# Attention scores by query-tile pairs: two packed 128-row products and four 32-row ones in row groups, reciprocals taken on columns

## The chip, the cores and the metric

The kernel runs on one core of a Trainium2 chip. The metric is the device time of one execution in microseconds (us), lower is better. Before the change it is 2180.84 us, the median of 3 runs (2180.51 to 2181.43).

The core's engines work side by side and meet at semaphores: PE (TensorE) multiplies matrices into PSUM, DVE (VectorE) and ACT (ScalarE) work element by element, POOL (GpSimd) does side work, and SP (SyncE) issues DMAs. Each engine takes its instructions in the order in which they are written.

## The reference

Two layers; each mixes tokens by attention and a convolution and then runs a gated FFN. Sequence 1024, model width 1024, 8 heads. The change is in the attention, whose score of a query and a key has a part of 64 dimensions of its own for each head and a rotary part of 32 dimensions whose key is shared by all heads.

```python
        q = (c_q @ w_uq[l].astype(h.dtype)).reshape(b, s, MLA_HEADS, MLA_NOPE_DIM + MLA_ROPE_DIM)
        q_nope = q[..., :MLA_NOPE_DIM]
        q_rope = _apply_rope(q[..., MLA_NOPE_DIM:], cos_h, sin_h)
        ...
        k_nope = kv[..., :MLA_NOPE_DIM]
        v = kv[..., MLA_NOPE_DIM:]
        k_rope = _apply_rope(p[..., o2:o3], cos, sin)
        y_attn = _mla_attention(q_nope, q_rope, k_nope, k_rope, v)
...
        sc = (jnp.einsum("bqhd,bkhd->bhqk", qn, k_nope)
              + jnp.einsum("bqhr,bkr->bhqk", qr, k_rope))
        p = jax.nn.softmax(sc.astype(jnp.float32) * scale, axis=-1).astype(v.dtype)
        return jnp.einsum("bhqk,bkhd->bqhd", p, v)
```

## The kernel before

Each layer has three stages: `project` (all input projections, rotary embedding, a part of the convolution), `attention`, and `feed` (output projection and FFN). Both layers run the same code, so every place below occurs twice in the program.

**Number format.** To come near float32, a float32 operand is split into an upper and a lower float16 half, and a product is made of three: upper by upper, upper by lower, lower by upper. In the tiles of a head, `q` and `k`, of shape (128, 2, 1024), index 0 and 1 of the middle dimension are the two halves; partitions 0 to 63 hold the head's own part, 64 to 95 the rotary part.

**Tiling of the attention.** A head has 8 query tiles of 128 rows, numbered n = 0 to 63 over the 8 heads. For a tile, `scores` (L1810 on) writes a PSUM tile `s` of 128x1024 (two banks; there are two such tiles) with 6 products of 96 rows by 512 columns (L1818); DVE takes the negated row maximum `mx` (L1820); `expo` lets ACT write the exponentials `p` with the row sums into `sums` (L1828). For every pair of tiles `turn` transposes `p` on PE in blocks of 128x128 into four PSUM tiles `t`, c = 0 to 3, of two blocks for each query tile (L1858); ACT writes the upper half `pt` of each (L1860), DVE the lower half (L1861). A group is two pairs; `values` multiplies its `pt` by the values into a PSUM tile `o`: in steps c = 0 to 3 two full products each (L1880), and with the last step 8 products of 64 columns (L1885) for the lower halves, which go into two column halves of PE. ACT and DVE then write `o` out as `yt` (L1891, L1892).

`sums` (L1901 on) handles the row sums when a head is done: PE transposes them into a PSUM tile `sr` of 8x128 (L1903), DVE takes the reciprocals (L1905), and SP writes them to DRAM and reads them back, spread over 64 partitions (L1906, L1907), for a later multiplication on POOL.

`o`, `t`, `sr` and the value projection's `pv` all come from a ring of four PSUM banks. A new tile in a bank waits until the tile before it in that bank has been read.

**Order.** The program is written out by hand in the order of each engine's queue: the loop over n emits the value products that are due at n, `turn(n)`, `scores(n + 2)`, `expo(n + 1)`, and then what `agenda[n]` holds (side work: late convolution taps, `sums`, casts). So PE works two tiles ahead of the exponentials and one pair ahead of the transposes. The eight value projections (`rows`, L1794, 6 products each) stand among the first tiles, as `ROWS`, `ROW_AT` and `ROW_LATE` say, each followed by two ACT and two DVE writes (L1804, L1807).

**How the operands reach the tiles.** `project` writes the split queries and keys to DRAM (`qd`, `qrd`, `kd`, `krd`) and `load_head` reads a head's tiles back, all on SP's queue (line L153, `move`). Head 0 (`DIRECT = 1`) is copied straight from the SBUF tiles, the rotary query parts `qr` (two tiles, one for each half of the 32 dimensions, heads on partitions) among them. `spills` holds the DRAM writes back until the second query projection; then they are issued one after another, and the loads of head 1 and head 2 stand behind them in SP's queue.

## Time and profile before

| what | value |
|---|---|
| median of 3 runs | 2180.84 us |
| span of the profiled execution, first to last instruction | 2179.0 us |
| busy PE / DVE / ACT / POOL | 2169.7 / 1844.7 / 1456.6 / 537.2 us |
| attention of layer 0, first `s` product to last | 200.07 to about 386.7 us |
| attention of layer 1, first `s` product to last | 1280.91 to 1467.2 us (start of the last) |
| DVE `mx` (L1820) | 128 times, mean 1211 ns |
| ACT `p` (L1828) | 128 times, mean 1120 ns, and 210 ns to read the sums |
| PE `s` (L1818), `t` (L1858) | 768 and 1024 products |

A matmul's duration in the trace is from its start to its modelled end; matmuls that follow each other overlap, so what one costs PE is read from the distance of the starts, or from the chain of work that ended last, which counts overlapping work once. Times are us from the start of the span.

### The profile page before, as it was taken

The page shows a single profiled execution, that of the slowest core. Times are in us where ns is not written, and L with a number is a line of the kernel's source. Part 1 is how long each engine was busy: PE and PEld are TensorE (multiplying, and loading weights), DVE is VectorE, ACT ScalarE, POOL GpSimd, SP SyncE. Part 2 cuts the span into 40 slices and gives each one's busy share as a digit, 9 for nine tenths or more (in the row PEclk, how much of TensorE's full clock was granted, in tenths as well). Part 3 has the DMA queues.
Part 4 walks back from the last instruction along what each step waited for, and adds up shares of the span by engine and source line. Part 5 has one row for each costly group of instructions (what it writes and reads, how often), then busy time and mean ns, then how long its engine had stood idle before and what let it go on. Part 6 is the DMA issues. An engine that isn't in the chain of part 4 may idle for free.

```text
span 2179.0 us, 29766 instructions
## 1 busy us (share of the span) xinstructions
PE 2169.7 (100%) x10722; PEld 1260.7 (58%) x10722; DVE 1844.7 (85%) x2531; ACT 1456.6 (67%) x2183; POOL 537.2 (25%) x534
## 2 busy tenths in 40 slices
PE   9999999999999999999999999999999999999998
PEld 8887665754444444644488876667544444446445
DVE  6989999879998887887859789998898888878877
ACT  6455888746898886554623668886478888865544
POOL 1223777211111111000012355771112111110000
PEclk9999999999999999999999999999999999999999
DMA  6898878754688885554578986886646888856533
GB/s 195 184 187 212 164 152 171 245 163 104 149 244 259 222 261 145 193 178 151 166 177 164 188 207 134 159 186 200 175 100 164 261 241 242 241 141 218 182 111 122
DMA packets 163013, 400.96 MB, mean 184 GB/s; under 512 B 21888, under 2 KB 29936, under 8 KB 162864
## 3 DMA queue, kind: packets, MB, share of 16 engines
q0 software_dynamic: 62528, 145.89, 36.4%
q1 hardware_dynamic: 100048, 252.63, 33.8%
q8 instruction: 84, 1.38, 0.3%
q10 hardware_dynamic: 288, 0.53, 0.1%
q14 instruction: 65, 0.53, 0.1%
HBM read 270.75 MB, written 69.66 MB: 156 GB/s over the span
## 4 chain that ended last, share of the span: by engine, by line
PE 98%; ACT 1%; DVE 1%; issue 0%; DMA 0%; DVEq 0%; ACTq 0%
PE p L1306 36%; PE pd L1551 18%; PE po L1026 7%; PE s L1818 7%; PE t L1858 5%; PE pq L245 3%; PE pa L245 3%; PE o L1880 2%; PE pkv L245 2%; PE pg L245 2%; PE pg L564 2%; PE pn L245 2%; PE o L1885 1%; PE pv L1794 1%; PE pk L245 1%; PE pa L564 1%
## 5 line engine op out<-in xcount | busy, mean ns | idle before, releaser
L1306 PE MATMUL p<-b,w 128*128 128x512 f16 x3696 | 800.0, 379 | 0.2
L1306 PEld LDWEIGHTS <-w 128*128 128x128 f16 x3696 | 358.7, 98 | 431.9 <-issue 0.8
L1551 PE MATMUL pd<-ab,wd 128*128 128x512 f16 (+2 forms) x1920 | 404.2, 373 | 0.0
L1196 POOL DMA_DIRECT2D wu<-in_w_up x176 | 152.2, 879 | 770.2 <-DVE w L1270 581.5
L1551 PEld LDWEIGHTS <-wd 128*128 128x128 f16 x1656 | 161.9, 98 | 179.4 <-issue 0.5
L1818 PE MATMUL s<-k,q 96*128 96x512 f16 x768 | 186.9, 379 | 0.0
L1270 DVE SCALAR_TENSOR_TENSOR w<-wu,wf,w 128x512 f16<-128x512 f32 (+1 forms) x216 | 177.2, 834 | 3.6 <-ACT w L1267 3.6
L1861 DVE SCALAR_TENSOR_TENSOR pt<-t,pt 128x512 f16<-128x512 f32 x256 | 163.0, 676 | 10.0 <-ACT pt L1860 9.0
L1267 ACT ACTIVATE w<-wu,wf 128x512 f16<-128x512 f32 (+1 forms) x216 | 164.8, 781 | 0.1
L1860 ACT ACTIVATE pt<-t 128x512 f16<-128x512 f32 x256 | 139.1, 596 | 32.0 <-PE t L1858 30.0
L1820 DVE TENSOR_REDUCE mx<-s 128x1 f32<-128x1024 f32 x128 | 155.0, 1211 | 1.0 <-PE s L1818 1.0
L1540 ACT ACTIVATE ab<-ac,ds 128x512 f16<-128x512 f32 x108 | 75.5, 717 | 108.7 <-DVE ac L1455 73.0
L1828 ACT ACTIVATE p<-s,mx 128x1024 f32<-128x1024 f32 x128 | 143.3, 1120 | 2.2 <-DVE mx L1820 1.8
L2039 DVE SCALAR_TENSOR_TENSOR conv<-gate,par,conv 128x1009 f32<-128x1009 f32 (+14 forms) x110 | 139.9, 1274 | 3.1 <-ACT conv L659 0.4
L2056 POOL TENSOR_SCALAR late<-gate,par 128x1019 f32<-128x1019 f32 (+13 forms) x99 | 135.5, 1368 | 27.2 <-PE pn L245 13.9
L1858 PE MATMUL t<-ident,p 128*128 128x128 f32 x1024 | 136.6, 275 | 0.9 <-ACT p L1828 0.6
L1858 PEld LDWEIGHTS t<-ident,p 128*128 128x128 f32 x1024 | 116.8, 141 | 34.8 <-issue 7.4
L1766 DVE SCALAR_TENSOR_TENSOR o<-zg,par,o 128x1023 f32<-128x1023 f32 x88 | 112.7, 1281 | 8.9 <-ACT o L1760 7.4
L1314 DVE SCALAR_TENSOR_TENSOR zg<-p,wf,zg 128x512 f32<-128x512 f32 x72 | 54.0, 750 | 71.2 <-PE p L1306 61.6
L1766 DVE SCALAR_TENSOR_TENSOR v<-zv,par,v 128x1023 f32<-128x1023 f32 x88 | 112.1, 1276 | 0.0
L1818 PEld LDWEIGHTS <-q 96*128 96x128 f16 x768 | 74.0, 97 | 64.6 <-issue 2.1
L1541 DVE SCALAR_TENSOR_TENSOR ab<-ac,ds,ab 128x512 f16<-128x512 f32 x108 | 79.9, 748 | 19.2 <-ACT ab L1540 19.2
(2179 smaller groups left out, 3814.1 us busy)
## 6 DMA issues: line engine op xcount, KB each, us to landing
wu<-in_w_up SPq DMA_DIRECT2D x98, 512.0 KB
wu<-in_w_up POOLq DMA_DIRECT2D x176, 256.0 KB, 4.8
sd<-in_w_down SPq DMA_DIRECT2D x44, 512.0 KB
ws<-sd SPq DMA_DIRECT2D x44, 512.0 KB
act<-v SPq DMA_DIRECT2D x36, 512.0 KB
ac<-act SPq DMA_DIRECT2D x72, 256.0 KB
wo<-in_w_o POOLq DMA_DIRECT2D x32, 256.0 KB, 7.7
x_mix<-y SPq DMA_DIRECT2D x32, 256.0 KB
```

Of the source, the lines that this page charges most:

```text
L245: nc.tensor.matmul(ps[:, HALVES[c]], w, x[:, HALVES[c]], start=(k == 0 and s == 0), stop=(k == n - 1 and s == 2))
L1026: self.nc.tensor.matmul(ps, p[:, sl], q[:, cs], start=(k == 0 and t == 0), stop=(k == 3 and t == 2))
L1196: nc.gpsimd.dma_start(out=dst, in_=src, accum_op=ALU.add)
L1267: nc.scalar.activation(out=t, in_=src, func=AF.Copy, scale=scale[f])
L1270: nc.vector.scalar_tensor_tensor(out=t, in0=src, scalar=scale[f], in1=hi, op0=ALU.mult, op1=ALU.subtract)
L1306: nc.tensor.matmul(ps, w[p][:, k * 128:(k + 1) * 128], b[:, q], start=(i in (1, 5, 2) and k == 0 and t == 0), stop=(k == 3 and t == 2), sk ...
L1551: nc.tensor.matmul(ps[t, m][:, cs], w[i, j][p][:, m * 128:(m + 1) * 128], b[:, q, cs], start=(i in (1, 5, 2) and j == 0 and s == 0), stop= ...
L1766: self.nc.vector.scalar_tensor_tensor(out=o[:, a:b], in0=z[:, at + a:at + b], scalar=self.par[l][:, tap:tap + 1], in1=o[:, a:b], op0=ALU.m ...
L1818: nc.tensor.matmul(ps[:, cs], q[0:96, i, qs], k[0:96, j, cs], start=(s == 0), stop=(s == 2))
L1820: nc.vector.tensor_reduce(out=mx, in_=ps, op=ALU.max, axis=AX.X, negate=True)
L1858: nc.tensor.transpose(tp[:, i, qi * 128:(qi + 1) * 128], st["p"][2 * qp + qi][:, kt * 128:(kt + 1) * 128], self.ident)
L1861: nc.vector.scalar_tensor_tensor(out=lo, in0=tp, scalar=P_SCALE, in1=hi, op0=ALU.mult, op1=ALU.subtract)
```

## The change

**The scores.** With three products of 96 rows, a score needs 288 rows. The change lays the same 288 rows out as 128 + 128 + 32. In `q[:, 0]` and `k[:, 0]` stand the upper half of the query's own part twice, against the upper and the lower half of the key; in `q[:, 1]` and `k[:, 1]` the lower half of the own part against the key's upper half (64 rows), and the upper half of the rotary part twice, against the two halves of the rotary key (64 rows). The rest is the lower half of the rotary query against the upper half of the rotary key: 32 rows. Its operands are put on four groups of 32 partitions: `qc` (shared by two heads) holds the query's part four times, `kc` the key's columns 0 to 511 in groups 0 and 2 and 512 to 1023 in groups 1 and 3. The new `scores` handles a pair of tiles: 4 products for the first tile, four 32-row products (two tiles by two column halves, each in its own row group and its own PSUM bank), and, later, 4 products for the second tile. A pair thus has 8 products of 128 rows and 4 of 32 rows where it had 12 of 96 rows.

**The order.** The loop runs over pairs. In an iteration PE gets: value products, first part of the next pair's scores with the four 32-row products, the transposes c = 0, 1, 3, the second tile's scores, value products, the transposes c = 2. The DVE and ACT halves of `turn` (`lower`, `upper`), the maximum (`largest`) and `expo` are placed between them one by one. At the start the value projections stand in three groups around the first pair.

**The reciprocals.** `inverses` takes them on the 128x8 tile of sums before the transposition; ACT copies the transposed tile out of PSUM.

**The operands.** Head 0 takes 12 small copies of rotary parts instead of 2, and one more of its own part; the rotary queries are written to DRAM by head and half in 32 pieces instead of 2; `load_head` issues 12 DMAs instead of 5.

```diff
-        qrd = self.dp.tile([2, HEADS, HALF, 2, T], F16, name=f"qrd{l}")
+        qrd = self.dp.tile([2, HEADS, ROPE, T], F16, name=f"qrd{l}")
...
+            st["kc"] = self.blk(f"kc{l}", F16, (128, 512))
+            for r in range(4):
+                self.move(st["kc"][r * ROPE:(r + 1) * ROPE], krd[0][:, HALVES[r % 2]])
...
                 for h in range(DIRECT):
-                    self.move(heads[h][0][NOPE + i * HALF:NOPE + (i + 1) * HALF], hl[h * HALF:(h + 1) * HALF])
-                spills.append((qrd[i].rearrange("h d p t -> (h d) p t"), hl))
+                    for r, (t, p) in enumerate([(heads[h][0][:, 1], 0)] * 2 + [(heads[h][2][:, h % 2], 1)] * 4):
+                        at = i * HALF + (NOPE + r * ROPE if p == 0 else (r - 2) * ROPE)
+                        self.move(t[at:at + HALF], hl[h * HALF:(h + 1) * HALF, p])
+                for p in range(2):
+                    for h in range(HEADS):
+                        spills.append((qrd[p, h, i * HALF:(i + 1) * HALF], hl[h * HALF:(h + 1) * HALF, p]))
...
+        self.move(q[NOPE:128, 0], qd[h][:, 0])
+        for p in range(2):
+            self.move(k[p * NOPE:(p + 1) * NOPE, 0], kd[h][:, p])
+            self.move(q[NOPE + p * ROPE:NOPE + (p + 1) * ROPE, 1], qrd[0, h])
+        self.move(k[0:NOPE, 1], kd[h][:, 0])
+        self.move(k[NOPE:128, 1], krd.rearrange("p d t -> (p d) t"))
+        for r in range(4):
+            self.move(qc[r * ROPE:(r + 1) * ROPE, h % 2], qrd[1, h])
...
-            for s, (i, j) in enumerate(((0, 0), (0, 1), (1, 0))):
-                for cs in HALVES:
-                    nc.tensor.matmul(ps[:, cs], q[0:96, i, qs], k[0:96, j, cs], start=(s == 0), stop=(s == 2))
+            def whole(e):
+                for i in range(2):
+                    for cs in HALVES:
+                        nc.tensor.matmul(two[e][:, cs], q[:, i, at[e]], k[:, i, cs], start=(i == 0 and e == 0),
+                                         stop=(i == 1 and e == 1), skip_group_check=True)
+
+            def rest():
+                for e in range(2):
+                    for c in range(2):
+                        r = slice((2 * e + c) * ROPE, (2 * e + c + 1) * ROPE)
+                        nc.tensor.matmul(two[e][:, HALVES[c]], qc[r, h % 2, at[e]], kc[r], start=(e == 1),
+                                         stop=(e == 0), skip_group_check=True)
...
+        def inverses(h):
+            nc.vector.reciprocal(out=state[h]["sums"], in_=state[h]["sums"])
...
-            nc.vector.reciprocal(out=rs, in_=pr)
+            nc.scalar.copy(out=rs, in_=pr)
...
+        for pair in range(total // 2 - 1):
+            n, nxt = 2 * pair + 1, pair + 1
+            products(n)
+            begin(nxt)
+            turn(pair, 0)
+            upper(pair, 0)
+            turn(pair, 1)
+            upper(pair, 1)
+            largest(2 * nxt)
+            ends = [rows(tt) for tt in ROWS_LATE.get(n, ())]
+            turn(pair, 3)
+            upper(pair, 3)
+            second.pop(nxt)()
+            lower(pair, 0)
+            largest(2 * nxt + 1)
+            expo(2 * nxt)
+            lower(pair, 1)
...
+            others(n)
+            products(n + 1)
...
+            turn(pair, 2)
+            upper(pair, 2)
+            expo(2 * nxt + 1)
+            lower(pair, 2)
+            lower(pair, 3)
...
+            others(n + 1)
```

Three places show how the queues move. First DVE, head 2 of layer 0, from the maximum of tile 2 to that of tile 4. `mx_2_2` is the maximum of head 2, tile 2; `t_2_03` is pair 0's transposed block c = 3; `pt_10` and `pt_11` are lower halves. Before:

```order
L1820 TENSOR_REDUCE mx_2_2_2260<-s_2_2_2253 128x1
L1861 SCALAR_TENSOR_TENSOR pt_10_2282<-t_2_00_2276,pt_00_2281 128x2x256
L1861 SCALAR_TENSOR_TENSOR pt_10_2282<-t_2_01_2287,pt_00_2281 128x2x256
L1820 TENSOR_REDUCE mx_2_3_2301<-s_2_3_2294 128x1
L1861 SCALAR_TENSOR_TENSOR pt_11_2284<-t_2_02_2310,pt_01_2283 128x2x256
L1861 SCALAR_TENSOR_TENSOR pt_11_2284<-t_2_03_2317,pt_01_2283 128x2x256
L1820 TENSOR_REDUCE mx_2_4_2331<-s_2_4_2324 128x1
```

The same place on DVE after the change (L1854 is the maximum, L1892 the lower half, L1920 `yt`, L1931 the reciprocals):

```order
L1854 TENSOR_REDUCE mx_2_2_2366<-s_2_2_2326 128x1
L1892 SCALAR_TENSOR_TENSOR pt_10_2356<-t_2_00_2350,pt_00_2355 128x2x256
L1854 TENSOR_REDUCE mx_2_3_2379<-s_2_3_2327 128x1
L1892 SCALAR_TENSOR_TENSOR pt_10_2356<-t_2_01_2360,pt_00_2355 128x2x256
L1892 SCALAR_TENSOR_TENSOR pt_11_2358<-t_2_02_2389,pt_01_2357 128x2x256
L1892 SCALAR_TENSOR_TENSOR pt_11_2358<-t_2_03_2368,pt_01_2357 128x2x256
L1920 SCALAR_TENSOR_TENSOR yt_0_1880<-o_1_1_2308,sc_85,yt_0_1880 64x512
L1931 RECIPROCAL sums_1_1974<-sums_1_1974 128x8
L1854 TENSOR_REDUCE mx_2_4_2434<-s_2_4_2412 128x1
```

The second maximum of a pair now stands between the lower halves of c = 0 and c = 1, and the lower half of c = 1 behind it. Second, PE at the transposition of the sums `sr_1`, also in head 2. Before, with the last score product of tile 6 ahead of it:

```order
L1858 MATMUL t_2_12_2380<-ident,p_2_3_2333 128x128 x2
L1858 MATMUL t_2_13_2387<-ident,p_2_2_2303 128x128 x2
L1858 MATMUL t_2_13_2387<-ident,p_2_3_2333 128x128 x2
L1818 LDWEIGHTS q_2_1978
L1818 MATMUL s_2_6_2394<-k_2_1979,q_2_1978 128x512
...
L1903 MATMUL sr_1_2408<-ident,sums_1_1900 8x128
```

After (L1836 are 128-row score products, L1908 value products, L1880 transposes):

```order
L1836 MATMUL s_2_5_2413<-k_2_2045,q_2_2044 128x512
L1908 LDWEIGHTS v_0_1652
L1908 MATMUL o_2_0_2457<-pt_00_2355,v_0_1652 128x512
...
L1880 MATMUL t_2_12_2460<-ident,p_2_2_2381 128x128 x2
L1880 MATMUL t_2_12_2460<-ident,p_2_3_2395 128x128 x2
L1935 MATMUL sr_1_2473<-ident,sums_1_1974 8x128
```

Before, six score products stood between the pair's last transposes and `sr`; now `sr` follows the transposes at once, three steps behind the second tile's scores. In both, `sr_1` takes the bank of `t_2_11`, so it waits for DVE's lower half of c = 1. Third, SP's queue from head 0's rotary copies to head 1's loads. Before:

```order
L153 DMA q_0_1324<-qr_0_1486 16x2048
L153 DMA q_0_1324<-qr_1_1487 16x2048
L153 DMA q_0_1324<-qns_0_1511 64x2048
L153 DMA qrd_81<-qr_0_1486 128x2048
L153 DMA qrd_81<-qr_1_1487 128x2048
L153 DMA qd_80<-qns_0_1511 128x2048
...
L153 DMA qd_80<-qns_3_1585 128x2048
L153 DMA q_1_1694<-qd_80 64x2048
L153 DMA q_1_1694<-qrd_81 16x2048 x2
L153 DMA k_1_1695<-kd_82 64x2048
L153 DMA k_1_1695<-krd_83 32x2048
```

After (`qr` is the rotary query in SBUF, `qns` the head's own part, `qrd` and `qd` their places in DRAM):

```order
L150 DMA q_0_1330<-qr_0_1495 16x1024 x2
L150 DMA qc_0_1329<-qr_0_1495 16x1024 x4
L150 DMA q_0_1330<-qr_1_1496 16x1024 x2
L150 DMA qc_0_1329<-qr_1_1496 16x1024 x4
L150 DMA q_0_1330<-qns_0_1520 64x2048
L150 DMA q_0_1330<-qns_0_1520 64x1024
L150 DMA qrd_81<-qr_0_1495 16x1024 x16
L150 DMA qrd_81<-qr_1_1496 16x1024 x16
L150 DMA qd_80<-qns_0_1520 128x2048
...
L150 DMA q_1_1759<-qd_80 64x2048
L150 DMA qc_0_1329<-qrd_81 32x1024 x4
```

Between the first copy for head 0 and the last load for head 1 there were 14 DMAs; there are now 62.

More of the change, by code (lines that the diff above doesn't have):

```diff
@@ L2012, in attention, with others, begin @@
+        def others(n):
             for f in agenda.pop(n, ()):
                 f()
-            if n == total - 1:
-                early(1, range(2))
-            if n == total:
-                values(2 * HEADS - 1, 0, n)
-                values(2 * HEADS - 1, 1, n)
-                early(1, range(2, 3))
-                values(2 * HEADS - 1, 2, n)
-                values(2 * HEADS - 1, 3, n)
+        def begin(pair):
+            h, p = divmod(pair, 4)
+            if h >= HEADS:
+                return
+            if p == 0:
+                state[h] = {"sums": self.cp.tile([128, 8], F32, name=f"sums{l}_{h}", tag="sums", bufs=3),
+                            "s": {}, "p": {}, "pt": {}, "qk": loaded.pop(h)}
+            second[pair] = scores(pair)
+            if p == 1 and h + 1 < HEADS and h + 1 not in loaded:
+                loaded[h + 1] = load(h + 1)
@@ new lines, in each @@
+        def each(pair, f, *e):
+            if pair < total // 2:
+                f(*e)
+        for tt in ROWS_FIRST:
+            rows(tt)()
+        begin(0)
+        ends = [rows(tt) for tt in ROWS_SECOND]
+        largest(0)
+        second.pop(0)()
+        expo(0)
+        for f in ends:
+            f()
+        largest(1)
+        ends = [rows(tt) for tt in ROWS_THIRD]
+        expo(1)
+        for f in ends:
+            f()
+        others(-1)
+        others(0)
+        for pair in range(total // 2 - 1):
[15 more added lines that the diff above has]
+            lower(pair, 1)
+            for f in ends:
+                f()
+            others(n)
+            products(n + 1)
+            ends = [rows(tt) for tt in ROWS_LATE.get(n + 1, ())]
+            turn(pair, 2)
[3 more added lines that the diff above has]
+            lower(pair, 3)
+            for f in ends:
+                f()
+            others(n + 1)
+            for qi in range(2):
+                state[pair // 4]["p"].pop(2 * (pair % 4) + qi)
@@ L2022, in attention @@
+        pair = total // 2 - 1
+        early(0, range(3))
+        for c in range(4):
+            turn(pair, c)
+            upper(pair, c)
+            lower(pair, c)
+            if c % 2:
+                others(total - 1 + c // 2)
+            if c == 1:
+                early(1, range(2))
+        g = 2 * HEADS - 1
+        values(g, 0, total)
+        values(g, 1, total)
+        early(1, range(2, 3))
+        values(g, 2, total)
+        values(g, 3, total)
         for m in range(2):
```

123 lines of the change are left out of this document (50 added, 73 removed).

## The prediction

> **What bounds the kernel now.** I read the page first, for the engine that ends the work, then the two attention stages by windows, then the chain of waits inside one of them.
>
> ```profile
> PE 2169.7 (100%) x10722; PEld 1260.7 (58%) x10722; DVE 1844.7 (85%) x2531; ACT 1456.6 (67%) x2183; POOL 537.2 (25%) x534
> PE 98%; ACT 1%; DVE 1%; issue 0%; DMA 0%; DVEq 0%; ACTq 0%
> ```
>
> The second line is the chain that ended last: 98% of the span is PE's own work. The windows (us of the stretch, then busy time of PE, PEld, DVE, ACT, POOL, granted clock, DMA share, GB/s) are the start and the middle of layer 0's attention:
>
> ```profile
> 216.00:237.00 21.00, 20.71 (x128) 12.57 (x127) 19.36 (x26) 17.19 (x32) 18.06 (x16) 1.00 0.87 167
> 237.00:370.00 133.00, 133.00 (x829) 80.14 (x828) 121.00 (x156) 109.39 (x195) 96.89 (x82) 1.00 0.80 160
> ```
>
> PE has no gap in 133 us, at the full clock; DVE is busy 121.0 of them (91%). So time leaves this stage only by less work on PE, and only until DVE, or the order in which the engines hand work to each other, becomes the limit. The chain of waits (start, us, what) shows the price of each step on PE, overlaps counted once:
>
> ```profile
> 300.89 1.30 PE s L1818 x6
> ...
> 304.90 0.43 PE o L1880 x2
> 305.33 0.87 PE t L1858 x8
> 306.20 1.30 PE s L1818 x6
> 307.50 0.43 PE o L1880 x2
> 307.93 0.98 PE o L1885 x8
> 308.92 1.02 PE t L1858 x8
> 309.94 1.30 PE s L1818 x6
> ...
> 312.54 1.30 PE s L1818 x6
> ```
>
> One group (two pairs of tiles) takes 312.54 - 300.89 = 11.65 us. A score product of 96 rows costs 1.30/6 = 0.217 us, a value product of 128 rows 0.43/2 = 0.217: the number of rows makes no difference. A transpose costs 0.87/8 = 0.109.
>
> **What the packing saves.** Per pair 12 products of 0.217 become 8 of 0.217 and a group of four with 32 rows. The trace has no 32-row product. The nearest row is L1885: eight products that each use half of PE's columns, in 0.98 us, where eight in sequence would take 1.74. So two halves ran together (4 x 0.217 = 0.87), with 0.11 us lost beside them, and the transposes right behind took 1.02 instead of 0.87: 0.15 more. Changing the division of PE costs 0.26 us a visit here. With the four 32-row products side by side the group costs 0.217 + 0.26 = 0.48 instead of 0.87: 0.39 saved, over 64 pairs **-25.0 us**. Below, a free change of division would save 0.65 a pair, 41.6 in all. Above, four products in sequence and the same change cost 1.13, 0.26 more than now, +16.6 in all. I take 0.39, since the row shows both the overlap and the loss.
>
> The Trainium skill, "TensorEngine Tiling (Array Packing)", Key Properties, says that a change of tiling mode drains TensorE; that speaks against visits as short as these, and the trace agrees, with 0.11 and 0.15 us around L1885. By the skill's "TensorE: Matmul & The Clock Gate", Part 3, four row tiles of 32 rows were measured 3.07 times as fast as in sequence; by that figure the group would be an estimated 4 x 0.217 / 3.07 = 0.28 instead of 0.217, and the sum 4 us higher. No run here shows it yet.
>
> **What the new order adds: two waits on PE.** There are still only two score tiles in PSUM, and now a pair fills both. Counted from E, the end of the second tile's four products:
>
> ```profile
> 306.04 1.46 PE L1818 MATMUL s<-k,q 96*128 96x512 f16 x6
> ...
> 307.67 1.21 DVE L1820 TENSOR_REDUCE mx<-s 128x1 f32<-128x1024 f32 x1
> ```
>
> E of the products in the chain above is 307.50; the maximum starts at 307.67, 0.17 later, and takes 1.21. From a maximum to PE the way leads over the exponential; it lay on the critical chain once, at the start:
>
> ```profile
> 217.37 1.28 DVE pt L1861 x2
> 218.65 1.14 DVE mx L1820
> ...
> 221.13 0.87 PE t L1858 x6
> ...
> 224.61 1.30 PE s L1818 x6
> ```
>
> The maximum has ended at 219.79, PE goes on at 221.13: 1.34 us. So the second tile is free for new scores at E + 0.17 + 1.21 + 1.34 = E + 2.72. That is what two of the next 32-row products wait for (the ones that write the second tile). PE's work before them is two value products (0.43), four transposes (0.44), two value products (0.43), four scores (0.87), the change of division (0.11): 2.28. PE stalls 0.44 us, and everything behind waits with it, since the queue is in order. In every other pair the 8 half products (0.98) stand there too and hide it. So it counts in 16 of a layer's 32 pairs, less 2 at the start and 7 in which the next wait has already taken the time: 7 x 0.44 x 2 layers = **+6.2 us**.
>
> The second wait is that of `sr` for its bank. The tile ahead of it is freed by the lower half of c = 1, which now stands behind the second maximum on DVE: 0.17 + 1.14 (maximum to the next instruction, row 218.65) + 0.68 (L1861 below) + 0.16 (the chain counts a product from the end of the one before; the scores that it has at 306.20 start at 306.04) = E + 2.15. PE has only 0.43 + 0.44 = 0.87 to do before it. It stalls 1.28 us; before, six score products (1.30) stood in between and hid this.
>
> ```profile
> L1861 DVE SCALAR_TENSOR_TENSOR pt<-t,pt 128x512 f16<-128x512 f32 x256 | 163.0, 676 | 10.0 <-ACT pt L1860 9.0
> L1905 DVE RECIPROCAL rs<-sr 8x128 f32<-8x128 f32 x14 | 13.1, 934 | 0.0
> ```
>
> L1905 gives the number of times, 14: 14 x 1.28 = **+17.9 us**. Queued behind `sr` are value products and the next pair's scores, so nothing makes it up. The bounds of both waits are zero, if DVE or ACT come earlier than in my sum, and twice these values. Together they take back nearly all of the 25.0.
>
> The reciprocals themselves leave DVE: 14 x 0.93 = 13.0 us less work there, for 14 that are short, 8 values in a row instead of 128. While PE or the handover limits, DVE's 9% of slack covers them, so I count nothing; were DVE the limit, it would be -13. ACT's 14 new copies of an 8x128 tile are smaller than any L1860 (0.6 us) and have ACT's slack for cover (109.4 of 133 busy); without it they cost up to 8 us.
>
> **The start.** Before, PE ran through it with tiles staggered one by one:
>
> ```profile
> 196.15 4.08 PE pv L1794 x18
> ...
> 204.22 2.74 PE pv L1794 x12
> ```
>
> ```profile
> 200.63 2.44 DVE L1807 SCALAR_TENSOR_TENSOR v<-pv,sc,v 128x256 f16<-128x256 f32 x6
> 206.21 1.63 ACT L1804 ACTIVATE v<-pv,sc 128x256 f16<-128x256 f32 x4
> 207.07 1.67 DVE L1807 SCALAR_TENSOR_TENSOR v<-pv,sc,v 128x256 f16<-128x256 f32 x4 [0.96 <-ACT v L1804]
> ```
>
> Now DVE has, behind tile 0's maximum (203.07 to 204.28, after the x6 row), the lower halves of two value projections, which wait for ACT's upper halves, which stand behind tile 0's exponential (to about 205.4). As in the last two rows that is 0.86 and 1.67 us more: tile 1's maximum starts at about 208.0 and frees PE at 208.0 + 1.21 + 1.34 = 210.55. PE, from 200.23: scores and group 0.87 + 0.48, 12 projections 2.74, scores 0.87, 12 projections 2.74, scores 0.87 = 208.8. It stalls 1.7. The next pair goes the same way with two more projections (maxima at about 212.9 and 214.7, PE free at 217.3 against 216.0): 0.5 and 0.8. About 3.0 us a layer: **+6.0**. Below zero is excluded, as PE had no more than 0.29 us of gaps here to win; above, 5 a layer.
>
> **SP's queue.** PE's timeline has the first scores of each layer, SP's (start, us, what it issues) the DMAs around them, and the list of what SP waits for (us in total, times, longest us) in a window of head 1, one landing:
>
> ```profile
> 200.07 1.25 PE L1818 MATMUL s<-k,q 96*128 96x512 f16 x5
> 1280.91 1.25 PE L1818 MATMUL s<-k,q 96*128 96x512 f16 x5
> ```
>
> ```profile
> 189.66 1.62 SPq L153 DMA_DIRECT2D q<-qr  x2
> 192.45 1.27 SPq L153 DMA_DIRECT2D qrd<-qr  x2
> 201.17 0.49 SPq L153 DMA_DIRECT2D q<-qd  x1
> 208.98 0.76 SPq L153 DMA_DIRECT2D k<-krd  x1
> 1268.84 1.64 SPq L153 DMA_DIRECT2D q<-qr  x2
> ```
>
> ```profile
> SPq L1907 <- DMA sd<-rs: 2.9, 1, 2.9
> ```
>
> The writes to `qrd` take 1.27/2 = 0.63 us per issue. From `q<-qd` to `k<-krd` there are ten loads in 201.17 to 209.74, 0.86 each, with DMA busy (share 0.87). A transfer lands 2.9 us after SP is ready again, some 3.3 after it started. From 189.66 there are now 12 copies (7.6), 2 (1.3), 32 writes (20.2), 4 (2.5) and 12 loads (7.6): the last load is issued at 228.2 and lands near 231.4. Head 1's first scores were at 224.61 with 8 score tiles before them; in the new order value products and half products (1.41) come first, three groups have saved 1.2 and the start has cost 3.0: 227.8, and the 32-row operands, loaded last, are wanted 0.9 later. PE stalls 2.7 us. In layer 1, SP starts 1.66 us earlier relative to the first score (1280.91 - 1268.84 = 12.07 ahead, instead of 200.07 - 189.66 = 10.41): 1.1. Loads of 0.86 would add 12 x 0.23 = 2.8 to both. I take between 3.8 and 9.4: **+5**, and from zero (issues of 0.55 or less) to +32 (all 62 issues of 0.86, 14 more in each layer). Later heads have 20 us of lead for 12 issues, and DMA's share of 0.80 in the middle leaves room; the cost is nothing there.
>
> **The sum**: -25.0 + 6.2 + 17.9 + 6.0 + 5 = +10.1 us on the span of 2179.0: 2189.1. The median is 1.84 above the span, so **2190.9, say 2191 us**.
>
> **Rivals.** (1) *Shorter waits*: the handovers above come from rows in which other work lay between, and half of the two waits would be -12.0: 2179; with none and loads in time 2162. For it: DVE gets 0.93 back at each head. Against it: the chain of a maximum, an exponential and PE is made of durations alone. (2) *Operands late*: all issues at 0.86, +32 instead of +5: 2218. For it: layer 1's loads of before. Against it: the 32 writes are small. It decides once an issue takes over 0.55 us; below that the loads are in time. (3) *No overlap of the 32-row products*: 41.6 more, of which the 6.2 of the first wait is absorbed: 2226. Then the change does not do what it says. For it: no row with row groups. Against it: L1885. (4) *The waits are right and the loads in time*: 2186.
>
> **How the numbers follow.** Around 2191, with (4): 0.44. Shorter waits: 0.17 under 2176.5, and 0.23 between that and 2185.2, where the waits are a little shorter and the loads in time. Late operands 0.10, no overlap 0.06. Within 0.2% (4.4 us, about what a measurement tells from no change) is 2176.5 to 2185.2. Faster 0.17, same 0.23, slower 0.60. The range reaches from 2172 (most of the shorter waits) to 2218 (late operands); the likeliest case alone holds 2185 to 2202.
>
> **What would show it.** Right: in the middle of the attention a group takes 11.6 to 11.8 us as before, PE has gaps ended by DVE's lower half ahead of `sr` and by ACT's `p` ahead of the 32-row products, and the first scores of head 1 end a gap that a DMA ended. The four 32-row products start within some ns of each other. Wrong: no gap on PE and a group of about 10.9 (rival 1); the four 0.2 us apart (rival 3); gaps that a maximum ends where PE had enough to do.

## The result and the profile after

The changed kernel takes 2234.18 us (median of 4 runs, 2232.64 to 2236.86), the kernel before 2181.14 us in the same comparison: 1.0244 times as long, 95% interval 1.0229 to 1.0258. That is 53 us more, where 10 were forecast; the direction was right, the size lies outside the range. The profiled execution's span is 2232.5 us.

The page's line of busy times, the chain that ended last, and the group of the 128-row score products (busy us, mean ns of one, idle us just before them and what ended most of that):

```profile
PE 2164.8 (97%) x10722; PEld 1243.0 (56%) x10722; DVE 1842.1 (83%) x2531; ACT 1454.5 (65%) x2197; POOL 536.4 (24%) x534
PE 86%; ACT 5%; DVE 4%; DMA 3%; issue 2%; SPq 1%; DVEq 0%; ACTq 0%
L1836 PE MATMUL s<-k,q 128*128 128x512 f16 x512 | 134.3, 384 | 31.8 <-DMA k<-kd 26.6
```

PE has hardly less to do than before (2169.7 us), and the chain is no longer PE's alone. One releaser stands out: DMA, 26.6 us, ahead of score products. The same two windows as before (us of the stretch, then busy time of PE, PEld, DVE, ACT, POOL, granted clock, DMA share, GB/s):

```profile
216.00:237.00 21.00, 12.03 (x76) 6.62 (x74) 13.52 (x19) 12.00 (x24) 16.64 (x15) 0.88 1.02 241
237.00:370.00 133.00, 117.72 (x746) 66.60 (x747) 105.49 (x136) 95.80 (x178) 79.19 (x66) 0.94 0.79 168
```

In the first, PE works 12.03 of 21 us, its clock is no longer full, and DMA is fully busy. The list of what PE waited for in layer 0 from the start of the attention on (us in total, times, longest us) names the places:

```profile
PE s L1836 <- DMA k<-kd: 13.7, 1, 13.7
PE sr L1935 <- DVE pt L1892: 6.9, 6, 1.2
PE s L1843 <- ACT p L1862: 3.6, 10, 1.2
PE s L1836 <- DMA k<-krd: 1.8, 1, 1.8
PE sr L1935 <- DVE sums L1931: 1.2, 1, 1.2
PE s L1843 <- DMA qc<-qrd: 1.1, 3, 0.5
```

Both forecast waits are there: `sr` at seven heads, six times for DVE's lower half and once for DVE's reciprocals (`sums`), and the 32-row products for the exponential. Above them stands one wait of 13.7 us for the operands of head 1, which the forecast had at 2.7.

**The steady state.** PE's timeline in head 2 (start, us, what; idle before it in brackets) shows each of the small terms once:

```profile
273.29 1.04 PE L1836 MATMUL s<-k,q 128*128 128x512 f16 x4
274.26 0.39 PE L1843 MATMUL s<-kc,qc 32*128 32x512 f16 x4
274.58 1.53 PE L1880 MATMUL t<-ident,p 128*128 128x128 f32 x12
...
278.12 1.03 PE L1836 MATMUL s<-k,q 128*128 128x512 f16 x4
279.08 0.39 PE L1843 MATMUL s<-kc,qc 32*128 32x512 f16 x2
279.64 0.39 PE L1843 MATMUL s<-kc,qc 32*128 32x512 f16 x2 [0.16 <-ACT p L1862]
...
284.57 1.04 PE L1836 MATMUL s<-k,q 128*128 128x512 f16 x4
...
290.40 0.27 PE L1935 MATMUL sr<-ident,sums 128*8 128x128 f32 x1 [1.16 <-DVE pt L1892]
290.51 0.59 PE L1908 MATMUL o<-pt,v 128*128 128x512 f16 x2
290.94 1.03 PE L1836 MATMUL s<-k,q 128*128 128x512 f16 x4
...
296.84 0.61 PE L1836 MATMUL s<-k,q 128*128 128x512 f16 x2
```

The four 32-row products are one entry of 0.39 us, so they run side by side, and 0.32 us after their start the transposes begin. The first pair takes 278.12 - 273.29 = 4.83 us, the fourth (with the 8 half products) 296.84 - 290.94 = 5.90: a group without waits is 10.73 us where it was 11.65. The second pair has its second two 32-row products 0.56 us late. (The idle time that the entry shows is smaller, 0.16, since a product's end is modelled late; what a wait costs is read from the starts.) The third pair has the wait at `sr`, 1.3 us by the starts; with the product itself and a slower start of the transposes ahead of it the pair takes 290.94 - 284.57 = 6.37 us, 1.54 more than the first. A whole head takes 296.84 - 273.29 = 23.55 us, before 23.31. So in the steady state saving and waits nearly cancel, as forecast.

**The start of head 1.** SP's timeline (start, us, what it issues) and the chain (start, us, what) show where the 43 us come from:

```profile
198.22 23.70 SPq L150 DMA_DIRECT2D qrd<-qr  x32
221.97 4.53 SPq L150 DMA_DIRECT2D qd<-qns  x4
227.31 1.99 SPq L150 DMA_DIRECT2D q<-qd  x2
...
240.79 2.78 SPq L150 DMA_DIRECT2D qc<-qrd  x4
```

```profile
227.31 13.46 DMA q<-qd
...
242.90 6.40 DMA qc<-qrd
```

The first load for head 1 is issued at 227.31 and has landed 13.46 us later; the last is issued at 242.90 and lands 6.40 later. In the kernel before, the ten loads of two heads were issued from 201.17 on, in 8.6 us. From PE's timeline of both layers: head 1's first score waits 13.70 and 12.85 us, and from there to head 2's first score it is 30.57 and 32.80 us instead of 23.5. Together 20.8 and 22.2 us, 43 of the 53.

### The profile page after: what moved, and what is told of

Read it like the earlier page. It is cut to its first block, busy times and chain, and to the rows that moved or that the text cites. A ratio compares the mean times of both kernels' runs of the same rounds, so it can differ in the third digit from the quotient of the medians.

```text
span 2232.5 us, 30063 instructions
## 1 busy us (share of the span) xinstructions
PE 2164.8 (97%) x10722; PEld 1243.0 (56%) x10722; DVE 1842.1 (83%) x2531; ACT 1454.5 (65%) x2197; POOL 536.4 (24%) x534
## 4 chain that ended last, share of the span: by engine, by line
PE 86%; ACT 5%; DVE 4%; DMA 3%; issue 2%; SPq 1%; DVEq 0%; ACTq 0%
PE p L1314 35%; PE pd L1559 18%; PE po L1034 7%; PE t L1880 3%; PE pq L242 3%; PE pa L242 3%; ACT p L1862 2%; PE s L1836 2%; PE pkv L242 2%; PE pg L242 2%; PE pg L561 2%; ACT pt L1888 2%; DVE mx L1854 1%; DMA q<-qd 1%; PE o L1908 1%
## 5 line engine op out<-in xcount | busy, mean ns | idle before, releaser
L1854 DVE TENSOR_REDUCE mx<-s 128x1 f32<-128x1024 f32 x128 | 155.6, 1216 | 64.3 <-PE s L1843 47.8
L1892 DVE SCALAR_TENSOR_TENSOR pt<-t,pt 128x512 f16<-128x512 f32 x256 | 164.4, 681 | 9.1 <-ACT pt L1888 7.9
L1836 PE MATMUL s<-k,q 128*128 128x512 f16 x512 | 134.3, 384 | 31.8 <-DMA k<-kd 26.6
L1880 PE MATMUL t<-ident,p 128*128 128x128 f32 x1024 | 140.9, 282 | 0.9 <-DVE pt L1892 0.4
L1880 PEld LDWEIGHTS t<-ident,p 128*128 128x128 f32 x1024 | 116.7, 143 | 31.5 <-issue 13.2
L1836 PEld LDWEIGHTS <-q 128*128 128x128 f16 x512 | 47.6, 98 | 85.0 <-issue 47.4
```

Source lines behind the costliest of these rows:

```text
L1836: nc.tensor.matmul(two[e][:, cs], q[:, i, at[e]], k[:, i, cs], start=(i == 0 and e == 0), stop=(i == 1 and e == 1), skip_group_check=True)
L1854: nc.vector.tensor_reduce(out=mx, in_=st["s"][qt], op=ALU.max, axis=AX.X, negate=True)
L1880: nc.tensor.transpose(tp[:, i, qi * 128:(qi + 1) * 128], st["p"][2 * qp + qi][:, kt * 128:(kt + 1) * 128], self.ident)
L1892: nc.vector.scalar_tensor_tensor(out=lo, in0=tps.pop((pair, c)), scalar=P_SCALE, in1=hi, op0=ALU.mult, op1=ALU.subtract)
```

## The experiments

The theory after the result: the loads were late because of SP's long queue. Its rival: the transfers are slow, whatever their place. Each run below is given with its ratio to the kernel before, which was measured beside it (medians of 2181.15 to 2181.36 us).

### 1. The 32 writes joined into 4

```diff
-                    for h in range(HEADS):
-                        spills.append((qrd[p, h, i * HALF:(i + 1) * HALF], hl[h * HALF:(h + 1) * HALF, p]))
+                    spills.append((qrd[p][:, i * HALF:(i + 1) * HALF], hl[:, p]))
```

> The changed kernel with its 32 writes of rotary queries to DRAM joined into 4, the same bytes in the same pieces of 2 KB. Theory A, the length of SP's queue: the 32 writes held it for 23.7 us (198.22 to 221.92), 28 fewer issues let head 1's loads start some 20 us earlier, the waits of 16.6 and 17.5 us for head 1's operands and the slow clock behind them go, and the time falls by about 40 us to about 2192; the stalls at the transposed sums (1.16 each) and at the 32-row products stay. Theory B, the transfers: 1.25 MB of operands a head instead of 0.75, with DMA over 100% busy, are late wherever they are issued; the waits stay above 10 us a layer and the time above 2215.

Measured: 2215.62 us, 1.0157 (1.0142 to 1.0173). 18.6 of the 40 us went: neither theory alone. The time lies at theory B's edge, but PE's waits for operands are 6.0 and 9.2 us in the two layers, below its 10. SP's timeline of this run:

```profile
198.30 4.75 SPq L150 DMA_DIRECT2D qrd<-qr  x4
203.09 7.87 SPq L150 DMA_DIRECT2D qd<-qns  x4
215.19 1.93 SPq L150 DMA_DIRECT2D q<-qd  x2
```

The `qrd` writes take 4.75 us instead of 23.70, but the four writes behind them now take 7.87 instead of 4.53, and SP, from 210.96 on, waits 4.2 us for their landing. The count of the issues was half of the matter; something makes each transfer slow.

### 2. The kernel before with its 2 writes split into 32

```diff
-                spills.append((qrd[i].rearrange("h d p t -> (h d) p t"), hl))
+                for p in range(2):
+                    for h in range(HEADS):
+                        spills.append((qrd[i, h, :, p], hl[h * HALF:(h + 1) * HALF, p]))
```

> The kernel before with nothing changed but its 2 writes of rotary queries to DRAM split into the 32 pieces that the changed kernel has. Theory A, the length of SP's queue: head 1's loads, issued from 201.17 before, start about 20 us later and are not there at 224.44; PE waits 5 to 14 us a layer, and the time is 2191 to 2215. Theory B, the transfers (larger loads and a busy DMA): these loads are as small as before and land in time, under 2184.

Measured: 2209.41 us, 1.0128 (1.0114 to 1.0141). What PE waited for in its layer 0:

```profile
PE s L1820 <- DMA k<-krd: 11.1, 1, 11.1
```

So these writes alone, with the old order and the old small loads, cost the kernel before 28 us, as theory A has it. The size of the new loads isn't needed to explain a wait of 11 us: it is enough that loads are issued 19 us later (at 220.20 instead of 201.17).

### 3. The sums transposed later

```diff
-                agenda[n + 1].append(lambda: sums(h, main, st, y, rb))
+                behind[n + 2].append(lambda: sums(h, main, st, y, rb))
...
             begin(nxt)
+            for f in behind.pop(n, ()):
+                f()
             turn(pair, 0)
```

> The changed kernel with the transposition of the sums moved on PE behind the next pair's first scores. Theory A, the step of the prediction: its 14 stalls of 1.16 us go, and with 14 x 1.16 = 16 us the time is about 2218; each of heads 2 to 6 takes 22.4 us from first score to first score instead of 23.5. Rival: the same wait comes back as a longer wait at the next 32-row products, which need the maximum and the exponential of the same pair; then half or less, 2226 to 2234, and heads of 22.9 to 23.5.

Measured: 2223.27 us, 1.0192 (1.0178 to 1.0206): 10.9 us less than the changed kernel, between the two. Heads 2 to 6 take 22.7 to 22.8 us. The waits at `sr` are gone, and in PE's timeline of the same head the pair that had it now waits at its 32-row products:

```profile
290.29 0.39 PE L1843 MATMUL s<-kc,qc 32*128 32x512 f16 x2
290.84 0.39 PE L1843 MATMUL s<-kc,qc 32*128 32x512 f16 x2 [0.17 <-ACT p L1862]
```

290.84 - 290.29 = 0.55. A wait of 1.3 us goes and one of 0.55 to 0.62 comes in its place, which is the rival in part.

### 4. The reciprocals alone, on the kernel before

```diff
-            nc.vector.reciprocal(out=rs, in_=pr)
+            nc.scalar.copy(out=rs, in_=pr)
...
+                inverses(h)
                 agenda[n + 1].append(lambda: sums(h, main, st, y, rb))
```

> The kernel before with the reciprocals alone changed: taken on the 128x8 sums before the transposition, and ACT copies the transposed tile. Prediction's step: 13 us less work on DVE, which has slack, and 14 more copies on ACT, which has slack too: 2180 to 2182, no difference. Rival: DVE's order limits somewhere, up to 13 us faster (2168); or ACT's copies stand ahead of something urgent, up to 8 us slower (2189).

Measured: 2182.21 us, 1.0005 (0.9996 to 1.0014): no difference. DVE's reciprocals fall from 934 to 192 ns each, 14 x 0.74 = 10.4 us of work that nobody waited for.

### 5. Without POOL's accumulating transfers

```diff
         if kind == "both":
             self.nc.gpsimd.tensor_tensor(out=y[:, lo:hi], in0=y[:, lo:hi], in1=p[:, lo:hi], op=ALU.add)
-        else:
-            self.nc.gpsimd.dma_start(out=y[:, lo:hi], in_=p[:, lo:hi], accum_op=ALU.add)
```

> The changed kernel without the accumulating transfers that POOL issues for the late convolution taps (those taps are left out of the sum; POOL's multiplications for them stay). In the kernel before they took 85% of the DMA engines at 158 GB/s in 230 to 250 us, where SP moved nothing. Theory A, contention: SP's issues of head 1's loads took 1.3 us each and landed 13.5 us later only because these transfers held the DMA engines; without them the issues take about 0.5, the loads land some 3 us after, and of the waits for head 1's operands (20.8 and 22.2 us with the slow clock) at most 3 a layer are left: 2191 to 2200. Theory B, the count of SP's issues alone: 62 issues by 0.63 still end at 228, and more bytes are slow by themselves: waits of 8 us and more a layer, 2208 to 2234.

Measured: 2193.89 us, 1.0058 (1.0043 to 1.0073), as contention has it. SP's timeline of this run, with the same 62 issues and the same bytes:

```profile
197.92 15.24 SPq L150 DMA_DIRECT2D qrd<-qr  x32
213.21 2.95 SPq L150 DMA_DIRECT2D qd<-qns  x4
```

15.24 us instead of 23.70, and no wait of PE for an operand in either layer.

### 6. PE kept busy during the wait

```diff
             products(n)
+            if nxt == 4:
+                idle, some = self.bank(f"idle{l}"), v[0][:, 0:2].rearrange("p h e d -> p (h e d)")
+                for i in range(56):
+                    nc.tensor.matmul(idle, v[1][:, 0, 0, :], some, start=(i == 0), stop=(i == 55))
             begin(nxt)
```

> The changed kernel with 56 products of 512 columns put on PE ahead of head 1's first scores, into a bank that nobody reads: 12.2 us of work inside the waits of 13.7 and 12.9 us. Theory A: the granted clock fell to 0.50 because PE stood idle, and the first pair of head 1 took some 4.3 us more in each layer from that; with PE busy the clock stays at 1.00 and the time is about 2225. Rival: the clock fell for another reason, or the first pair was slow only because its operands came late: 2232 to 2236.

Measured: 2234.36 us, 1.0248 (1.0231 to 1.0265): no gain, so the time falls to the rival. The windows tell more. First this run while the added products run, and after them, then the changed kernel without them:

```profile
228.00:240.00 12.00, 12.00 (x61) 5.35 (x58) 2.33 (x4) 1.82 (x4) 8.73 (x8) 1.00 1.03 248
244.00:252.00 8.00, 5.18 (x16) 2.52 (x17) 1.44 (x2) 0.60 (x1) 5.48 (x5) 0.58 1.07 245
```

```profile
230.00:234.00 4.00, 0.00 (x0) 0.00 (x0) 0.74 (x1) 0.03 (x1) 3.31 (x2) 0.77 1.05 272
234.00:242.00 8.00, 0.00 (x0) 0.00 (x0) 0.00 (x0) 0.00 (x0) 4.99 (x6) 0.50 1.04 241
```

With PE busy its clock stays at 1.00 although DMA is just as full; idle, it has fallen to 0.50 within some 5 us. That part of the theory holds. But the clock fell in this run too, a little later, in the shorter waits between the single operands, and the first pair's 32-row products followed the landings of `qc` one by one anyway. Most of the 4.3 us that the expectation put on the clock was such waiting. What the clock alone costs stays open; the 12 transposes behind it took 252.49 - 249.87 = 2.62 us in the changed kernel where 1.37 is usual.

### 7. Writes joined, sums later, and head 1 copied from SBUF

```diff
-DIRECT = 1
+DIRECT = 2
...
-                        self.move(t[at:at + HALF], hl[h * HALF:(h + 1) * HALF, p])
+                        copy = t[at:at + HALF], hl[h * HALF:(h + 1) * HALF, p]
+                        self.move(*copy) if h == 0 else spills.insert(0, copy)
```

> The changed kernel with the writes joined as in the first run, the sums later as in the third, and head 1 copied from SBUF as head 0 is, ahead of the writes, so that it waits for no DRAM. Theory A: the whole loss at head 1 (43 us in both layers) and the 10.9 us of the third run go: about 2180, and heads 2 to 6 at 22.74. Rival: the late operands only move to head 2, whose loads now meet POOL's transfers behind the same writes, or to head 0, whose copies are delayed: 2190 to 2215.

Measured: 2181.41 us, 1.0002 (0.9993 to 1.0011), as the theory has it; heads 2 to 6 of layer 0 take 22.7 to 22.8 us. Its ten executions lie between 2180.31 and 2185.18. The two losses are separate, and they add up: 43 and 10.9 are 53.9, and 52.8 went.

### 8. The 32-row products behind the first transposes

```diff
-            whole(0)
-            rest()
-            return lambda: whole(1)
+            whole(0)
+            return rest, lambda: whole(1)
...
             turn(pair, 0)
             upper(pair, 0)
+            second[nxt][0]()
             turn(pair, 1)
```

> The kernel of the seventh run with the four 32-row products behind the transposes of c = 0 instead of ahead of them. In the third run every second pair waited 0.55 to 0.62 us at those products for the exponential, 1.2 us a head. Theory A: four transposes (0.44) hide most of it, 0.15 a wait is left and heads take 21.9: 13 us less than the seventh run. Rival: the maximum of the pair's first tile comes 0.44 later too, DVE's queue and so the exponentials with it, and the waits stay: within 4 us of the seventh run.

Measured: 2180.98 us, 0.9998 (0.9989 to 1.0007), no difference to the seventh run: the rival. PE's waits in heads 1 to 6 of layer 0, of the seventh run and then of this one:

```profile
PE s L1844 <- ACT p L1863: 2.4, 12, 0.2
```

```profile
PE t L1880 <- ACT p L1862: 1.6, 6, 0.3
PE t L1880 <- DVE pt L1892: 1.3, 6, 0.2
```

The 32-row products wait no more; the transposes ahead of them do, six times for the exponential and six times for a bank that DVE's lower half frees, twelve as before.

### 9. POOL's taps listed later

```diff
-LATE_FROM = 0
+LATE_FROM = 8
```

> The changed kernel with POOL's late convolution taps started 8 tiles later (at tile 8 instead of tile 0) and packed closer behind that; nothing is left out. Theory A, contention with POOL's transfers: SP's writes and head 1's loads now run while POOL moves nothing, as in the fifth run; the waits for head 1's operands (20.8 and 22.2 us) fall to under 3 a layer and the time to 2191 to 2200, and up to 5 more if POOL's taps now end too late for what follows. Rival: without the taps left out altogether the same transfers meet the loads anyway, waits over 8 us a layer, 2210 to 2234.

Measured: 2219.56 us, 1.0176 (1.0162 to 1.0190). That is in the rival's range, but the run doesn't test what it was made for. POOL's timeline:

```profile
201.24 0.88 POOL L2146 DMA_DIRECT2D conv<-late  x1 [1.86 <-issue]
```

POOL's first accumulating transfer still starts at 201.24 (201.18 in the changed kernel). The table sets only the place in the program; POOL has its own queue and runs ahead. It is 14.6 us faster all the same. What differs in the traces: POOL waits twice for PE from 213 us on (1.91 and 1.31 us), its next transfers are issued at 216.68 and 223.90 instead of 214.77 and 220.66, and between 195 and 230 us its queue moves 3.00 MB instead of 3.55. That fits contention, but no run shows that all of the 14.6 us comes from it.

### 10. Tile 1's maximum ahead of the value projections' writes

```diff
         expo(0)
+        largest(1)
         for f in ends:
             f()
-        largest(1)
```

> The kernel of the seventh run with tile 1's maximum put ahead of the first writes of the value projections on DVE (two lines swapped). The prediction's step on the start: those writes wait for ACT and hold the maximum back by 2.5 us, and PE's 2.0 and 2.6 us at the second group of 32-row products come from that. Theory A: these waits go, 4 to 6 us less than the seventh run, about 2176. Rival: the projections' banks come free later instead and PE waits there, within 1.5 us of the seventh run.

Measured: 2175.69 us, 0.9982 (0.9973 to 0.9991), 5.7 less than the seventh run, by the medians. Seven of the eleven executions lie between 2174.89 and 2175.82, four between 2180.39 and 2182.71. What PE waited for at the 32-row products in layer 1's first pairs, in the seventh run and here:

```profile
PE s L1844 <- ACT p L1863: 2.9, 3, 2.2
```

```profile
PE s L1844 <- ACT p L1863: 0.8, 2, 0.6
```

The forecast's step on the start holds: the writes in front of the maximum made that stall. In the seventh run the clock also fell to 0.50 in 1294 to 1296 us, behind that stall; here it stays at 1.00. The trace is of an execution of 2181.76 us, one of the four. In it head 2 of layer 0 waits for its operands, which the seventh run does not:

```profile
PE s L1844 <- DMA qc<-qrd: 1.5, 3, 0.7
```

With another 0.7 us for `k` and a clock of 0.50 in 254 to 258 us, this takes back what the start gives. No trace shows one of the seven others, so that their operands come in time is likely but not shown.

### 11. POOL held for head 1's loads

```diff
-LATE_FROM = 0
+LATE_FROM = 8
...
+        held = lambda t: nc.gpsimd.tensor_scalar(out=t, in0=t, scalar1=1.0, scalar2=1.0, op0=ALU.mult, op1=ALU.mult)
+        agenda[8].append(lambda: held(state[0]["sums"][:, 7:8]))
```

> The changed kernel with POOL's late convolution taps held until tile 7's exponential (about 226 us instead of 201 in layer 0) by an operation that reads its row sum; nothing is left out. The run with the later start in the table did not hold POOL, which ran ahead in its own queue and began at 201 all the same. Theory A, contention with POOL's transfers: the 32 writes take 15 to 16 us as in the fifth run, head 1's loads are issued by 224 and land by 228, the waits for them are under 3 us a layer, 2191 to 2200 plus up to 5 for taps that end late. Rival: 62 issues and 1.25 MB are late by themselves, 2210 and more.

Measured: 2187.53 us, 1.0029 (1.0018 to 1.0040): 46.7 us less than the changed kernel, with all transfers kept. The run has the table of the ninth run and one operation more, which makes POOL wait; POOL's first transfer in layer 0 is now this one:

```profile
230.50 0.89 POOL L2148 DMA_DIRECT2D conv<-late  x1 [0.30 <-POOL late L2143]
```

SP's timeline, the loads of `qc` last:

```profile
198.23 15.26 SPq L150 DMA_DIRECT2D qrd<-qr  x32
213.54 2.95 SPq L150 DMA_DIRECT2D qd<-qns  x4
216.59 2.50 SPq L150 DMA_DIRECT2D q<-qd  x2
...
223.05 1.96 SPq L150 DMA_DIRECT2D qc<-qrd  x4
```

The issues are as fast as in the fifth run, and head 1's first score, at 228.42, waits for no operand. The gain is more than the theory asked for, since about 4 us of it come from the start: the second group of 32-row products is late by 1.02 us in layer 0 and 0.52 in layer 1, instead of 1.58 and 2.57, and layer 1 has no slower clock behind it. With POOL held, the three `qns` operations that DVE has ahead of layer 1's first maximum take 3.7 us instead of 5.8, and that maximum starts 2.0 us after PE's first score instead of 4.1.

### 12. Keys loaded ahead of queries

```diff
         q, k, qc = tiles = self.head_tiles(l, h)
+        for p in range(2):
+            self.move(k[p * NOPE:(p + 1) * NOPE, 0], kd[h][:, p])
+        self.move(k[0:NOPE, 1], kd[h][:, 0])
+        self.move(k[NOPE:128, 1], krd.rearrange("p d t -> (p d) t"))
         self.move(q[0:NOPE], qd[h])
         self.move(q[NOPE:128, 0], qd[h][:, 0])
         for p in range(2):
-            self.move(k[p * NOPE:(p + 1) * NOPE, 0], kd[h][:, p])
             self.move(q[NOPE + p * ROPE:NOPE + (p + 1) * ROPE, 1], qrd[0, h])
-        self.move(k[0:NOPE, 1], kd[h][:, 0])
-        self.move(k[NOPE:128, 1], krd.rearrange("p d t -> (p d) t"))
```

> The kernel of the tenth run with each head's four key loads issued ahead of its query loads. In the tenth run SP stood from 223.85 to 233.52 us behind the query writes while head 2's keys, long in DRAM, waited behind it; in some executions head 2's operands came 6.5 us late (2180 to 2183 instead of 2175). Theory A: the keys fill that gap, and all executions take 2174 to 2177. Rival: the DMA engines are full in any order, and some executions stay at 2180.

Measured: 2175.43 us, 0.9976 (0.9966 to 0.9987). Six of eight executions lie between 2175.05 and 2175.77, two at 2178.69 and 2180.07, where the tenth run had four of eleven above 2180. So theory A fails for two of eight. Whether the order of the keys did anything can't be told: two of eight against four of eleven is too few, and the medians are 0.26 us apart. The trace, of the execution of 2178.69 us, has no wait for a key, but 2.0 us of waits for `qc`, which is still loaded last. This version is 0.24% faster than the kernel before.

## Why the prediction was right in direction and wrong in size

| term of the sum | forecast | measured | from |
|---|---|---|---|
| packing | -25.0 | -29.4 | 32 groups of 10.73 instead of 11.65 us |
| wait at `sr` | +17.9 | +20.6 | 14 groups longer than 10.73 by 1.39 to 1.54 |
| wait at the 32-row products | +6.2 | +8.7 | per layer six of 0.55 to 0.62 and a last of 0.91 |
| the start | +6.0 | about +10 | second and third group of 32-row products late by 1.58 and 0.99 (layer 0), 2.57 and 0.98 (layer 1), smaller waits of 2.4, and 1.4 at the lower clock in layer 1 |
| loads of head 1 | +5 | +43 | 20.8 and 22.2 us |

The measured terms add up to about 52.9 of the 53 us.

**Packing, both waits, reciprocals: right.** The value taken for the four 32-row products was 0.48 us, and by the first pair it is 4.83 - 12 x 0.217 - 16 x 0.109 = 0.48. The 4.4 us beyond the forecast come from the 8 half products, which the sum left alone: they cost 5.90 - 4.83 = 1.07 in their new place behind value products and ahead of scores, where before, ahead of transposes, 11.65 - 32 x 0.217 - 32 x 0.109 = 1.22 was left for them. The chain of a maximum, an exponential and PE gave 0.44 where 0.55 to 0.62 is measured. The one over DVE's lower half gave 1.28 where the wait is 1.3 by the starts; the product `sr` itself (0.11) and the slower transposes ahead of it come on top in the table. At the seventh head `sr` waits for the reciprocals, a path that the prediction did not have, for about as long (1.2). Run 4 shows that DVE's reciprocals cost nothing before the change. Runs 3 and 8 add what the sum could not show: the two waits are one loop through DVE and ACT. Take one away, and a part of it comes back at the next handover.

**The start: right in mechanism, too small.** Run 10 shows the mechanism: the maximum behind the projections' writes. The prediction had both layers alike; layer 1 lost 5.9 us and layer 0 4.0. What it left out is in PE's timeline of layer 1 (start, us, what) and the window around it:

```profile
1317.96 0.61 PE L1843 MATMUL s<-kc,qc 32*128 32x512 f16 x2 [2.18 <-ACT p L1862]
1318.49 2.73 PE L1880 MATMUL t<-ident,p 128*128 128x128 f32 x12
```

```profile
1315.00:1320.00 5.00, 2.82 (x14) 1.71 (x12) 3.00 (x7) 3.02 (x7) 4.62 (x5) 0.76 1.08 203
```

The clock is 0.50 from 1318 to 1321 us, behind the wait, and the twelve transposes take 1321.06 - 1318.49 = 2.57 us instead of 1.37. And DVE reached layer 1's first maximum late beside POOL's work, as run 11 shows.

**SP's queue: the step that failed.** The prediction priced the writes at 0.63 us per issue and the landing at 3.3 us, with a row at 192 us and with the landing of `sd`, 8 rows of 128 numbers, and took +5 with +32 as the worst. At 192 us POOL's accumulating transfers had not begun; before the change the first was issued at 200.07. The 32 writes took 23.7 us instead of 20.2, the four writes behind them 4.5 instead of 2.5, head 1's twelve loads 16.3 (227.31 to 243.57) instead of 7.6, and the last landed after 6.4 instead of 3.3, the first after 13.5. So the price came from a moment ahead of POOL's transfers, from writes of another size (512 KB; the writes of 32 KB take 0.48 us each in runs 5 and 11, 0.74 beside POOL's transfers) and from the landing of a transfer of 4 KB, and the worst case raised the issues but left the landing at 3.3. What the runs showed in its place: from 201 us on POOL's transfers hold the engines, and the 28 more writes push head 1's loads into that time. Run 2 shows that the writes alone do it, run 5 that the loads are in time without POOL's transfers, run 11 that they are in time if these only begin later. How busy engines lengthen SP's issue itself, no run shows. So the late operands were the right mechanism, listed at one chance in ten; its price was too small, and its chance was given on the argument that the writes are small. Rival (4), the waits as computed and the loads in time, was put at 2186; run 11 is nearly that case: 2187.5. So the direction does not hang on the loads alone. That the two times are so close is partly luck: the packing gave 4.4 us more than forecast, and the two waits together took 5.2 more.

How the DMA engines were shared is in the lists of queues from 230 to 250 us (packets, MB, share of 16 engines; the first is POOL's, the second SP's), before the change and after:

```profile
q0 software_dynamic: 879, 3.13, 84.3%
```

```profile
q0 software_dynamic: 701, 2.53, 68.4%
q1 hardware_dynamic: 1072, 2.43, 37.4%
```

In this stretch POOL's transfers alone had 84.3% of the engines before; after, SP's loads are in it too, and the two queues together fill them.

The Trainium skill, "DMA: Bandwidth & Descriptors", section "Queues, rings and completion order", says that each DMA engine takes turns between the queues that have work for it. The trace agrees as far as it goes: while PE waited for SP's loads, POOL's queue still had 68.4% of the engines' time.

## What to carry to other kernels

Price a DMA by a row from the same moment of the program, with the same neighbours on the DMA engines; a row from a quiet moment gives neither the issue nor the landing. When a change adds issues ahead of a load, ask which stream of transfers the load is pushed into, and not only how long the issues take. An order between engines' queues exists only where one waits for the other: the table that listed POOL's work later left its first transfer where it was, since POOL waited for nobody there.

## What the hardware showed that was not expected

An issue on SP's queue has no fixed price. The same 32 writes of 32 KB took 15.2 to 15.3 us with POOL's transfers away (runs 5 and 11) and 23.7 beside them; of head 1's loads, those behind the first two took 0.44 to 0.58 us an issue in run 11, and the first five of them 1.23 to 1.42 in the changed kernel.

PE's granted clock went from 1.00 to 0.50 in the wait of 13.7 us and stayed there for the first work behind it; in run 6, with PE busy in the same stretch, it stayed at 1.00. The Trainium skill, "TensorE: Matmul & The Clock Gate", Part 1, says that an idle window of about 3.4 us halves the clock. The windows of the changed kernel agree: PE's last product started before 229 us, the mean of 230 to 234 is 0.77, and from 234 on it is 0.50. But a shorter gap was enough elsewhere: at the start of layer 1 PE stood still for 2.18 us, and the clock was 0.50 for some 3 us behind that. There the measurement decides: waits of about 2 us can cost the clock too.
